# Hybrid decoder block on one core: eight of the FFN ends' LayerNorm tiles by ScalarE and POOL instead of two VectorE passes

## The chip, the cores and the metric

The kernel runs on one core of a Trainium2 chip. The metric is the device time of one execution in microseconds, taken as the median of several runs. Before the change the runs took 2291.83, 2285.61 and 2290.1 us, so the median is 2290.1 us.

Five engines work side by side on the core, each through its own instructions in order: PE (TensorE, matmuls and transposes), DVE (VectorE), ACT (ScalarE), POOL (GpSimd) and SP (SyncE, which here only issues DMAs). They wait for each other through semaphores.

## The reference

One decoder block over 1024 tokens of width 1024, with 16 learned meta tokens ahead of them, all in float32:

```python
h = layer_norm(ALPHA * h + 0.5 * swiglu(h, ffn1_w_gate, ffn1_w_up, ffn1_w_down), ln1_g, ln1_b)
h = layer_norm(ALPHA * h + hybrid_mixer(h, w_in, conv_w, w_att_out, w_conv_out, w_o), ln2_g, ln2_b)
h = layer_norm(ALPHA * h + 0.5 * swiglu(h, ffn2_w_gate, ffn2_w_up, ffn2_w_down), ln3_g, ln3_b)
return h[:, 16:]

def layer_norm(x, g, b):
    xc = x - mean(x)
    return xc * rsqrt(mean(xc * xc) + 1e-5) * g + b

def swiglu(x, w_gate, w_up, w_down):
    return (silu(x @ w_gate) * (x @ w_up)) @ w_down
```

The change touches the LayerNorm behind the first FFN and the one behind the second; the LayerNorm behind the mixer (ln2) stays.

## The kernel before, in words

**Stages.** The program runs FFN 1, the mixer, FFN 2. Tokens are worked on in tiles of 128: eight tiles t0 to t7 of 1024 tokens in all, and in FFN 1 a ninth tile, t8, with the 16 rows that are left over because of the meta tokens. Each FFN has a gate/up part, whose hidden values go to DRAM (`hd1` and `hd`), and a down projection, `halves_down`, which reads them back. Every float32 matmul is three matmuls on split values (`chain`, L262 to L269: high by high, high by low, low by high).

**The down projection.** `halves_down` multiplies by halves, with seven products P1 to P7 instead of eight. The hidden width is taken in chunks. For each chunk, for each half `ip` of the columns, and for each product, it lays the hidden values into a tile `hl` by DMAs that SP issues (L555; `load` runs some products ahead), multiplies them with the weights into a PSUM bank (tags a, b, c), and adds the bank to the tile's accumulator `y` on DVE (L595; L593 in the last chunk, where the row sums for the norm are taken along). In the last chunk, `ip` = 0 works on two column blocks at once: the tiles t0 and t1 are finished with product P3, t4 and t5 with P4. For `ip` = 1 each block is done by itself: t2, t6, then t3, t7. "First two tiles of each half" are t0, t1 and t4, t5.

**The norm behind it.** When a tile's last accumulation is through, `done` is called: `finish` at FFN 1, `done3` at FFN 2. Both call `short_norm` (L236 to L252): nm, the negative mean, on DVE (L243); Square with the row sum on ACT (L244); Sqrt on ACT (L245), ahead of whose first use a function table is loaded; z = (y + nm) * g on DVE (L246); r = 1/sqrt on DVE (L247); y = z * r + b on DVE (L250). Both long DVE passes read two tensors of 128x1024 in SBUF.

**What follows the norm.** At FFN 1, `finish` stores the tile to `h1` (L1222, DMA on SP) and then turns it for the mixer (`to_stream`, `turn`): per half of its columns four transposes on PE into a PSUM bank (L190), a cast on ACT (L191), the low part on DVE (L192). `done` holds these back: with the call for one tile, the first half of the tile two calls earlier is turned. At FFN 2, `short_norm` itself issues the store to the output (L252, on SP); nothing on PE reads the result.

**The longer form.** `layer_norm` (L219 to L234) is there already for some tiles of the mixer's norm: after r it computes nr = nm * r on DVE (L231), y = y * r + nr on ACT (L232, Identity), and then y * g and y + b as two passes on engines handed in (L233, L234).

**Who sets the order.** Code is written as generators, and a scheduler then sets the order of each engine's instructions from the whole program, so a change in one place also moves its neighbours. At run time each engine, SP's DMA queue among them, takes its instructions strictly in that order.

Of the kernel before, what the change touches and what calls it, by code (L numbers as in the profile page):

```python
# [11 lines left out]
F32 = mybir.dt.float32  # L12
# [3 lines left out]
AF = mybir.ActivationFunctionType  # L16
OP = mybir.AluOpType
# [3 lines left out]
D = 1024  # L21
# [69 lines left out]
class Block:  # L91
# [128 lines left out]
    def layer_norm(self, y, p, sums, gb, eng, junk, eps=None):  # L220

        eps = self.eps if eps is None else eps
        nc = self.nc
        g, b = gb
        new = lambda n: self.small.tile([128, 1], F32, name=n, bufs=6)[:p]
        nm, sq, ve, r, nr = new("nm"), new("sq"), new("ve"), new("rstd"), new("nr")
        nc.vector.tensor_scalar(nm, sums[:p, 0:1], sums[:p, 1:2], -1.0 / D, op0=OP.add, op1=OP.mult)
        nc.scalar.activation(junk[:p], y[:p], AF.Square, bias=nm, accum_out=sq)
        nc.scalar.activation(ve, sq, AF.Sqrt, bias=eps[:p], scale=1.0 / D)
        nc.vector.reciprocal(r, ve)  # L230
        nc.vector.tensor_tensor(nr, nm, r, OP.mult)  # L231
        nc.scalar.activation(y[:p], y[:p], AF.Identity, bias=nr, scale=r)  # L232
        eng[0].tensor_tensor(y[:p], y[:p], g[:p], OP.mult)  # L233
        eng[1].tensor_tensor(y[:p], y[:p], b[:p], OP.add)  # L234

    def short_norm(self, y, p, sums, gb, junk, z, parts=1, dst=None, eps=None):  # L236

        eps = self.eps if eps is None else eps
        nc = self.nc
        g, b = gb  # L240
        new = lambda n: self.small.tile([128, 1], F32, name=n, bufs=6)[:p]
        nm, sq, ve, r = new("nm"), new("sq"), new("ve"), new("rstd")
        nc.vector.tensor_scalar(nm, sums[:p, 0:1], sums[:p, 1:2], -1.0 / D, op0=OP.add, op1=OP.mult)  # L243
        nc.scalar.activation(junk[:p], y[:p], AF.Square, bias=nm, accum_out=sq)  # L244
        nc.scalar.activation(ve, sq, AF.Sqrt, bias=eps[:p], scale=1.0 / D)  # L245
        nc.vector.scalar_tensor_tensor(z[:p], y[:p], nm, g[:p], op0=OP.add, op1=OP.mult)  # L246
        nc.vector.reciprocal(r, ve)  # L247
        for j in range(parts):
            sl = slice(D // parts * j, D // parts * (j + 1))
            nc.vector.scalar_tensor_tensor(y[:p, sl], z[:p, sl], r, b[:p, sl], op0=OP.mult, op1=OP.add)  # L250
            if dst is not None:
                nc.sync.dma_start(dst[:, sl], y[:p, sl])  # L252
# [865 lines left out]
    def first_ffn(self):  # L1118

        nc, a = self.nc, self.a  # L1120
# [13 lines left out]
        with ExitStack() as c1:  # L1134
# [6 lines left out]
            with ExitStack() as c5:  # L1141
# [8 lines left out]
                y = []  # L1150
                for t in range(NT + 2):
                    p = 128 if t < NT else 8
# [62 lines left out]
            def finish(t, y, sums):  # L1215

                p = 128 if t < NT else 16
                junk = self.lnp.tile([128, D], BF16, name="junk")
                self.short_norm(y, p, sums, self.gb1, junk, self.lnp.tile([128, D], F32, name="z"), eps=self.eps4)
                if t < NT:  # L1220
                    r0 = META if t == 0 else 0
                    nc.sync.dma_start(self.h1[cols[t] + r0 - META:cols[t] - META + 128, :], y[r0:])  # L1222
                else:
                    for i in range(2):
                        nc.sync.dma_start(self.h1[512 + WIDE * i - META:520 + WIDE * i - META, :], y[8 * i:8 * i + 8])
                yield
                for half in range(2):
                    if half:

                        yield  # L1230
                    if t < NT:
                        self.to_stream(y, cols[t], 128, "ba"[half], (half,))
                        continue
                    ps = self.ps("ba"[half])
                    psv = ps.rearrange("q (j c) -> q j c", j=4)
                    for j in range(4):
                        nc.tensor.transpose(psv[:, j, :16], y[:16, 512 * half + 128 * j:512 * half + 128 * j + 128],
                                            self.ident[:16, :16])
                    for i in range(2):
                        hi, lo = (v[:, 4 * half:4 * half + 4, 512 + WIDE * i:520 + WIDE * i] for v in both)  # L1240
                        S.copy(hi, psv[:, :, 8 * i:8 * i + 8])
                        V.tensor_tensor(lo, psv[:, :, 8 * i:8 * i + 8], hi.bitcast(F32), OP.subtract)

            def done(t, y, sums):
                later.append(finish(t, y, sums))
                next(later[-1])
                if len(later) > 2:
                    next(later[-3])
# [13 lines left out]
    def run(self, stop=None):  # L1262
        nc, tc, a = self.nc, self.tc, self.a
# [14 lines left out]
        with ExitStack() as c2:  # L1278
            ys = ExitStack()
            yp = self.pool(ys, "f2y", 1, "right")  # L1280
            with ExitStack() as c3:
# [3 lines left out]
                y = []  # L1285
# [4 lines left out]
                gb = self.load_ln(lambda: wp.tile([128, D], F32, name="gb", bufs=2), a["ln2_g"], a["ln2_b"])  # L1290
# [22 lines left out]
                for t, (col, p) in enumerate(real):  # L1313
                    sums = self.small.tile([128, 2], F32, name="sums", bufs=6)
# [16 lines left out]
            with ExitStack() as c4:  # L1331
                up = self.weights_left(c4, 2, 2, 2)
                sp = self.pool(c4, "ws", 2)
                hps = ExitStack()
                with ExitStack() as c5:
                    tp = self.pool(c5, "f2t")
                    o1, o2 = real[0][0], real[NT // 2][0]
                    st1 = (self.xh, self.xl)
                    X = {"11": [x[:, 0:4, o1:o1 + 512] for x in st1], "21": [x[:, 4:8, o1:o1 + 512] for x in st1],
                         "22": [x[:, 4:8, o2:o2 + 512] for x in st1], "T1": [x[:, 0:4, o2:o2 + 512] for x in st1]}  # L1340
                    for n in ("T2", "T3", "T4"):
                        X[n] = [tp.tile([128, 4, 512], F32R, name=f"{n}{x}") for x in "hl"]
                    st = ExitStack()

                    gate_up.send((up, sp, X))
                    for g in later[NT - 2:]:
                        next(gate_up)
                        next(gate_up)
                        next(g, None)
                    for t in range(NT // 2):  # L1350
                        for n, src in (("T1", y[t][:, :512]), ("T2", y[t + 4][:, 512:]), ("T3", y[t + 4][:, :512]),
                                       ("T4", y[t][:, 512:])):
                            self.turn(src, 128, *(x[:, :, 128 * t:128 * t + 128] for x in X[n]), "c")
                            if t:
                                next(gate_up)
                    self.show("x3")
                    ys.close()
                    self.hp = self.pool(hps, "f2hl", 4, "right")
                    down = self.halves_down(up, sp, self.hd, wd, lambda t: [(0, self.h1[128 * t:128 * t + 128, :])])
                    next(down)  # L1360
                    pending = gate_up.send((self.pool(st, "f2h", 5, "right"), down))

                pools = {"more": self.pool(c4, "f2more", 4), "y": self.pool(c4, "f2y2")}
                rs = ExitStack()

                def ending():
                    st.close()
                    pools["r"] = self.pool(rs, "f2r", 1, "right")
                    self.lnp = self.pool(rs, "f2ln", 1, "right")
                    self.gb3 = self.load_ln(lambda: self.lnp.tile([128, D], F32, name="gb", bufs=2), a["ln3_g"], a["ln3_b"])  # L1370

                def done3(t, y, sums):
                    junk = self.lnp.tile([128, D], BF16, name="junk")
                    dst = a["out"][0, 128 * t:128 * t + 128, :]
                    z = self.lnp.tile([128, D], F32, name="z")
                    self.short_norm(y, 128, sums, self.gb3, junk, z, 1 if t < 7 else 2, dst, self.eps4)

                down.send((pending, pools, ending, done3))
                rs.close()
                hps.close()  # L1380
# [46 lines left out]
```

## Time and profile before

| | |
|---|---|
| median of 3 runs | 2290.1 us |
| the execution in the profile | 2288.11 us |
| its span, first to last instruction | 2286.3 us |
| mean granted TensorE clock | 0.977 of full speed |
| PE busy | 2192.2 us |
| DVE busy | 1530.8 us |
| ACT busy | 894.7 us |
| POOL busy | 841.0 us |
| FFN 1's first norm of a tile (DVE, nm) | at 718.24 us |
| FFN 2's first norm of a tile (DVE, nm) | at 2249.48 us |

Times inside the profile are microseconds from the span's start. A row of a timeline has the start, the duration, the engine and line, the operation with its output and inputs, and in brackets the idle time before it and what ended that. A row of waits names the waiting engine with its tile and line, and behind the arrow the engine and line whose result came last. DMA instructions are issued on SP's queue, called SPq. Starts of pipelined instructions may lie before the end of the one ahead.

### The profile page before, as it was taken

To read this page: it belongs to the slowest core of one execution; us is meant where nothing else is said; L and a number is where in the kernel's file an instruction comes from. 1 tells how busy PE (TensorE), PEld (TensorE's weight loads), DVE (VectorE), ACT (ScalarE), POOL (GpSimd) and SP (SyncE) were. 2 spreads that over 40 slices of the span, in tenths; PEclk is the share of its full clock that TensorE was granted. 3 is DMA by queue.
4 is the path that set the end of the run, shared out by engine and by line. 5 is a ranking of instruction groups with operands and counts; after the bars stand their busy time and mean duration, and the time that the engine had idled before them with its cause. 6 is when DMAs were issued, how large, how long until landed. Compare 5 with 4: busy or idle time off the path is not lost.

```text
span 2286.3 us, 31567 instructions
## 1 busy us (share of the span) xinstructions
PE 2192.2 (96%) x11708; PEld 1861.9 (81%) x11708; DVE 1530.8 (67%) x2716; ACT 894.7 (39%) x1484; POOL 841.0 (37%) x573
## 2 busy tenths in 40 slices
PE   6999999999999898999999999999999999989997
PEld 5999999987777777899887777777788888867776
DVE  6456565565787648699997787635555555555787
ACT  4434444443112327233225676432444444343212
POOL 2454555563220201265443110214355464653320
PEclk7999999999999898999999999999999999999999
DMA  3435445369685344431224212631253535368784
GB/s 121 133 109 160 145 127 178 102 230 333 196 269 173 106 136 93 130 76 43 74 83 97 51 42 70 221 143 65 65 184 118 186 105 190 112 225 308 236 272 155
DMA packets 299685, 335.02 MB, mean 147 GB/s; under 512 B 20432, under 2 KB 227948, under 8 KB 299148
## 3 DMA queue, kind: packets, MB, share of 16 engines
q1 hardware_dynamic: 230508, 243.33, 33.9%
q10 hardware_dynamic: 52976, 80.76, 9.9%
q0 software_dynamic: 16048, 8.93, 2.1%
q8 instruction: 92, 1.51, 0.3%
q14 instruction: 61, 0.50, 0.1%
HBM read 220.19 MB, written 112.76 MB: 146 GB/s over the span
## 4 chain that ended last, share of the span: by engine, by line
PE 52%; DVE 3%; DMA 3%; POOL 1%; ACT 1%; issue 1%; SPq 0%; DVEq 0%; ACTq 0%; POOLq 0%
PE a L269 14%; PE c L269 7%; PE ps L171 6%; PE ps L170 6%; PE ps L169 6%; PE b L269 3%; PE pt L958 2%; PE ps L1322 1%; PE ps L1323 1%; PE ps L1321 1%; PE po L949 1%; PE sc L923 1%; PE po L950 1%; DMA raw<-in_ffn_w_down_dram 1%; PE acc L760 1%
## 5 line engine op out<-in xcount | busy, mean ns | idle before, releaser
L143 DVE TENSOR_TENSOR lo<-raw,hi 128x1024 fp32r<-128x1024 f32 (+1 forms) x176 | 194.3, 1118 | 177.3 <-ACT hi L142 174.2
L142 ACT CAST hi<-raw 128x1024 fp32r<-128x1024 f32 (+1 forms) x219 | 187.9, 872 | 298.0 <-PE ps L170 81.6
L169 PE MATMUL ps<-xh,hi 128*128 128x512 f32 (+2 forms) x664 | 248.7, 375 | 0.3 <-DVE t L677 0.3
L171 PE MATMUL ps<-xh,lo 128*128 128x512 f32 (+2 forms) x664 | 248.5, 374 | 0.0
L170 PE MATMUL ps<-xl,hi 128*128 128x512 f32 (+2 forms) x664 | 248.3, 374 | 0.0
L793 DVE TENSOR_SCALAR_CACHE_REDUCE junk<-sc,cand 128x1040 uint8<-128x1040 f32 (+6 forms) x217 | 182.2, 893 | 0.0
L269 PE MATMUL c<-xh,hi 128*128 128x260 f32 (+1 forms) x704 | 176.0, 311 | 0.8 <-DVE T3l L192 0.8
L269 PE MATMUL c<-xh,lo 128*128 128x260 f32 (+1 forms) x704 | 176.1, 311 | 0.0
L269 PE MATMUL c<-xl,hi 128*128 128x260 f32 (+1 forms) x704 | 176.0, 311 | 0.0
L143 POOL TENSOR_TENSOR lo<-raw,hi 128x1024 fp32r<-128x1024 f32 (+1 forms) x43 | 87.9, 2044 | 207.8 <-ACT hi L142 207.8
L269 PE MATMUL a<-xh,hl 128*128 128x512 f32 x416 | 145.3, 398 | 4.6 <-DVE y L595 2.9
L323 POOL TENSOR_TENSOR ws<-raw 128x512 f32<-128x512 f32 x40 | 53.7, 1343 | 260.4 <-DMA raw<-in_ffn_w_gate_dram 202.1
L170 PEld LDWEIGHTS ps<-xl,hi 128*128 128x128 f32 x664 | 126.1, 190 | 17.0
L169 PEld LDWEIGHTS ps<-xh,hi 128*128 128x128 f32 x664 | 126.0, 190 | 16.8 <-DVE t L677 0.5
L171 PEld LDWEIGHTS ps<-xh,lo 128*128 128x128 f32 x664 | 125.7, 189 | 16.5
L595 DVE TENSOR_TENSOR y<-a,y 128x512 f32<-128x512 f32 x152 | 101.3, 684 | 39.6 <-PE a L269 39.2
L269 PE MATMUL a<-hi,hl 128*128 128x512 f32 x288 | 107.9, 420 | 20.2 <-DMA hl<-hd 8.3
L269 PEld LDWEIGHTS c<-xh,hi 128*128 128x128 f32 x704 | 114.5, 188 | 9.0 <-DVE T3l L192 1.0
L269 PEld LDWEIGHTS c<-xl,hi 128*128 128x128 f32 x704 | 114.6, 188 | 7.7
L269 PEld LDWEIGHTS c<-xh,lo 128*128 128x128 f32 x704 | 114.4, 188 | 7.8
L143 DVE TENSOR_TENSOR lo<-ws,hi 128x1024 fp32r<-128x1024 f32 x54 | 109.7, 2032 | 4.6 <-ACT hi L142 3.2
L269 PEld LDWEIGHTS a<-xh,hl 128*128 128x128 f32 x416 | 78.4, 188 | 25.4 <-DVE y L595 4.2
(360 smaller groups left out, 5892.6 us busy)
## 6 DMA issues: line engine op xcount, KB each, us to landing
hl<-hd SPq DMA_DIRECT2D x280, 256.0 KB
hd<-hl ACTq DMA_DIRECT2D x154, 256.0 KB
hd<-hl ACTq DMA_DIRECT2D x77, 512.0 KB
raw<-in_ffn_w_gate_dram SPq DMA_DIRECT2D x44, 512.0 KB
raw<-in_ffn_w_up_dram SPq DMA_DIRECT2D x44, 512.0 KB
raw<-in_ffn_w_down_dram SPq DMA_DIRECT2D x44, 512.0 KB
raw<-in_w_in_dram SPq DMA_DIRECT2D x37, 512.0 KB
h<-y SPq DMA_DIRECT2D x15, 512.0 KB
```

The lines of the kernel that those rows point to most:

```text
L142: self.nc.scalar.copy(hi, src)
L143: lo_eng.tensor_tensor(lo, src, hi.bitcast(F32), OP.subtract)
L169: mm(out, wh, xh, start=start, stop=False)
L170: mm(out, wh, xl, start=False, stop=False)
L171: mm(out, wl, xh, start=False, stop=stop)
L269: self.nc.tensor.matmul(out, w, v, start=start and first, stop=last, skip_group_check=True)
L323: P.tensor_tensor(s[:, 512:], r2[:, :512], r2[:, 512:], OP.add)
L595: V.tensor_tensor(yv, ps, yv, OP.add)
L760: nc.tensor.matmul(ps[:, :n], q[:, h, :], self.ki1[:, o:o + n], start=True, stop=False)
L793: V.tensor_scalar(junk[:, :x.shape[1]], x, s, None, op0=OP.is_ge, op1=OP.add, accum_out=cnt[:, j:j + 1])
L923: nc.tensor.matmul(ps[:, :w], q[:, r, :], self.k1[:, g, o:o + w], start=True, stop=False)
L958: nc.tensor.transpose(pt[:kw, m * r:m * r + m], ps_[r][q0:, 128 * kb:128 * kb + kw], self.ident[q0:, q0:])
```

## The change

A new function, `side_norm`, computes the norm in the longer form with three differences: nr on ACT instead of DVE, both passes with the weight g and the bias b on POOL, and no tile z. `finish` and `done3` call it for t0, t1, t4 and t5, and the other tiles keep `short_norm`. At FFN 2 the store of such a tile is issued by `done3` itself, in one piece as before. Over the whole program DVE loses 16 instructions, ACT and POOL have 16 more each, and PE and SP keep their number.

```diff
--- before.py
+++ after.py
@@ -232,6 +232,21 @@
         nc.scalar.activation(y[:p], y[:p], AF.Identity, bias=nr, scale=r)
         eng[0].tensor_tensor(y[:p], y[:p], g[:p], OP.mult)
         eng[1].tensor_tensor(y[:p], y[:p], b[:p], OP.add)
+
+    def side_norm(self, y, p, sums, gb, junk, eps):
+
+        nc = self.nc
+        g, b = gb
+        new = lambda n: self.small.tile([128, 1], F32, name=n, bufs=6)[:p]
+        nm, sq, ve, r, nr = new("nm"), new("sq"), new("ve"), new("rstd"), new("nr")
+        nc.vector.tensor_scalar(nm, sums[:p, 0:1], sums[:p, 1:2], -1.0 / D, op0=OP.add, op1=OP.mult)
+        nc.scalar.activation(junk[:p], y[:p], AF.Square, bias=nm, accum_out=sq)
+        nc.scalar.activation(ve, sq, AF.Sqrt, bias=eps[:p], scale=1.0 / D)
+        nc.vector.reciprocal(r, ve)
+        nc.scalar.mul(nr, nm, r)
+        nc.scalar.activation(y[:p], y[:p], AF.Identity, bias=nr, scale=r)
+        nc.gpsimd.tensor_tensor(y[:p], y[:p], g[:p], OP.mult)
+        nc.gpsimd.tensor_tensor(y[:p], y[:p], b[:p], OP.add)
 
     def short_norm(self, y, p, sums, gb, junk, z, parts=1, dst=None, eps=None):
 
@@ -1216,7 +1231,10 @@
 
                 p = 128 if t < NT else 16
                 junk = self.lnp.tile([128, D], BF16, name="junk")
-                self.short_norm(y, p, sums, self.gb1, junk, self.lnp.tile([128, D], F32, name="z"), eps=self.eps4)
+                if t in (0, 1, 4, 5):
+                    self.side_norm(y, p, sums, self.gb1, junk, self.eps4)
+                else:
+                    self.short_norm(y, p, sums, self.gb1, junk, self.lnp.tile([128, D], F32, name="z"), eps=self.eps4)
                 if t < NT:
                     r0 = META if t == 0 else 0
                     nc.sync.dma_start(self.h1[cols[t] + r0 - META:cols[t] - META + 128, :], y[r0:])
@@ -1372,8 +1390,12 @@
                 def done3(t, y, sums):
                     junk = self.lnp.tile([128, D], BF16, name="junk")
                     dst = a["out"][0, 128 * t:128 * t + 128, :]
-                    z = self.lnp.tile([128, D], F32, name="z")
-                    self.short_norm(y, 128, sums, self.gb3, junk, z, 1 if t < 7 else 2, dst, self.eps4)
+                    if t in (0, 1, 4, 5):
+                        self.side_norm(y, 128, sums, self.gb3, junk, self.eps4)
+                        nc.sync.dma_start(dst, y)
+                    else:
+                        z = self.lnp.tile([128, D], F32, name="z")
+                        self.short_norm(y, 128, sums, self.gb3, junk, z, 1 if t < 7 else 2, dst, self.eps4)
 
                 down.send((pending, pools, ending, done3))
                 rs.close()
```

The new order is shown at three places. The first is PE at the end of FFN 1 before the change, around the first transposes of t0 (tile `y0_5559`, first half, into bank b; `ident` is the identity matrix, `hl` the hidden values, `a` and `c` banks):

```order
L269 MATMUL a_7302<-hi_6834,hl_7100 128x512
L269 MATMUL a_7302<-xh_58,hl_7100 128x512
L269 MATMUL a_7302<-xl_59,hl_7100 128x512
L269 MATMUL a_7302<-xh_58,hl_7100 128x512
L269 MATMUL c_7335<-xh_58,hl_7160 128x512
L190 MATMUL b_7265<-ident_60,y0_5559 128x128 x4
L269 MATMUL c_7335<-xl_59,hl_7160 128x512
L269 MATMUL c_7335<-xh_58,hl_7160 128x512 x2
```

The same place on PE with the change (line numbers are 15 higher, and bank a_7302 is now a_7310):

```order
L284 MATMUL c_7343<-xh_58,hl_7160 128x512
L284 MATMUL a_7474<-hi_6834,hl_7307 128x512
L284 MATMUL a_7474<-lo_6835,hl_7307 128x512
L190 MATMUL b_7271<-ident_60,y0_5559 128x128 x4
L284 MATMUL a_7310<-hi_6834,hl_7199 128x512
L284 MATMUL a_7310<-lo_6835,hl_7199 128x512
L284 MATMUL c_7343<-hi_6911,hl_7180 128x512
L284 MATMUL c_7343<-lo_6912,hl_7180 128x512
L284 MATMUL c_7343<-hi_6911,hl_7180 128x512
L284 MATMUL c_7343<-hi_6954,hl_7180 128x512
```

Counted from the first matmul on hl_7100 (the one behind the products on hl_7083), 7 matmuls stood ahead of t0's transposes before, and 20 stand there now. The second place is PE a little later in the new order. Nine matmuls behind t0's transposes stand t1's (tile `y1_5560`), and 30 matmuls behind those t4's and t5's (`hm` holds the hidden values of the ninth tile):

```order
L621 MATMUL b_7361<-hi_6954,hm_112 48x512
L621 MATMUL b_7361<-lo_6955,hm_112 48x512
L190 MATMUL b_7394<-ident_60,y4_5563 128x128 x4
L284 MATMUL a_7474<-xh_58,hl_7307 128x512
L284 MATMUL a_7474<-xl_59,hl_7307 128x512
L190 MATMUL b_7424<-ident_60,y5_5564 128x128 x4
L284 MATMUL a_7474<-xh_58,hl_7307 128x512
```

Counted in matmuls from the same start, the first transposes of t0, t1, t4 and t5 stood behind 7, 18, 53 and 56 before, and stand behind 20, 29, 59 and 61 now.

The third place is SP's queue at the end of FFN 2 before the change (`out_0_dram` is the output, y0 to y7 are the tiles, `hl` the loads for the last products):

```order
L252 DMA out_0_dram<-y4_18811 128x1024
L555 DMA hl_20469<-hd_87 128x2x128 x2
L555 DMA hl_20480<-hd_87 128x2x128 x2
L252 DMA out_0_dram<-y5_18812 128x1024
L252 DMA out_0_dram<-y2_18809 128x1024
L252 DMA out_0_dram<-y6_18813 128x1024
```

and with it:

```order
L1395 DMA out_0_dram<-y4_18819 128x1024
L570 DMA hl_20485<-hd_87 128x2x128
L1395 DMA out_0_dram<-y5_18820 128x1024
L267 DMA out_0_dram<-y2_18817 128x1024
L570 DMA hl_20496<-hd_87 128x2x128 x2
L267 DMA out_0_dram<-y6_18821 128x1024
```

Both loads of the last `hl` tile (20480 before, 20496 now), which feeds the last product of the kernel, have moved from ahead of t5's store to behind it and t2's.

## Rows read from the trace of the kernel before

**Rows 1.** Page, part 1: busy time and share of each engine

```profile
PE 2192.2 (96%) x11708; PEld 1861.9 (81%) x11708; DVE 1530.8 (67%) x2716; ACT 894.7 (39%) x1484; POOL 841.0 (37%) x573
```

**Rows 2.** Busy time (instructions) of PE, PEld, DVE, ACT, POOL; granted clock; DMA share; GB/s

```profile
720.00:735.00 15.00, 15.00 (x73) 10.73 (x73) 14.83 (x28) 6.47 (x13) 0.00 (x0) 1.00 0.79 246
2266.00:2278.00 12.00, 8.81 (x31) 6.45 (x29) 11.02 (x23) 4.18 (x8) 0.00 (x0) 0.86 0.32 131
```

**Rows 3.** PE waits at FFN 1's end, 735 to 771: us, times, longest us

```profile
PE a L190 <- DVE xl L192: 1.8, 2, 1.5
PE b L190 <- DVE y L250: 1.7, 1, 1.7
PE b L190 <- DVE xl L1242: 1.3, 1, 1.3
PE pt L650 <- DVE xl L192: 1.2, 1, 1.2
PE b L190 <- DVE y L593: 1.1, 1, 1.1
```

**Rows 4.** PE waits at FFN 2's end, 2233 to 2287

```profile
PE a L269 <- DVE y L595: 2.9, 2, 2.4
```

**Rows 5.** Timeline of DVE, FFN 1's end: start us, us, line, operation [idle]

```profile
718.49 1.28 DVE L246 SCALAR_TENSOR_TENSOR z<-y,nm,gb 128x1024 f32<-128x1024 f32 x1
...
721.57 1.29 DVE L250 SCALAR_TENSOR_TENSOR y<-z,rstd,gb 128x1024 f32<-128x1024 f32 x1
...
732.07 1.28 DVE L250 SCALAR_TENSOR_TENSOR y<-z,rstd,gb 128x1024 f32<-128x1024 f32 x1
```

**Rows 6.** Timeline of ACT, FFN 1's end

```profile
721.25 1.13 ACT L244 ACTIVATE junk<-y,nm 128x1024 bf16<-128x1024 f32 x1
...
722.50 0.29 ACT L245 ACTIVATE ve<-sq,eps 128x1 f32<-128x1 f32 x1
```

**Rows 7.** Lines L232 and L234: ns min/median/max, first and last start

```profile
L232 ACT ACTIVATE y<-y,nr,rstd x6: 1243/1244/1245, 1507.8 to 1565.3; 128x1024 f32<-128x1024 f32 x6
...
L234 POOL TENSOR_TENSOR y<-y,gb x6: 2403/2416/3262, 1511.1 to 1567.9; 128x1024 f32<-128x1024 f32 x6
```

**Rows 8.** Timeline of PE, FFN 1's end

```profile
721.89 0.40 PE L269 MATMUL a<-hi,hl 128*128 128x512 f32 x1
...
723.06 0.60 PE L190 MATMUL b<-ident,y 128*128 128x128 f32 x4
723.42 0.48 PE L269 MATMUL c<-xl,hl 128*128 128x512 f32 x1
```

**Rows 9.** Timeline of SP, FFN 2's end

```profile
2254.12 0.35 SPq L252 DMA_DIRECT2D out_dram<-y  x1
2254.57 2.33 SPq L555 DMA_DIRECT2D hl<-hd  x4
```

**Rows 10.** DMA issues: count, KB each, median us to landing

```profile
q<-qs POOLq DMA_DIRECT2D x16, 256.0 KB, 3.3
...
qi<-qis POOLq DMA_DIRECT2D x7, 512.0 KB, 4.6
```

**Rows 11.** Timeline of POOL, 1570 to 1580

```profile
1574.42 1.29 POOL L1307 TENSOR_TENSOR y<-y,y 128x512 f32<-128x512 f32 x1
1575.79 2.16 POOL L1308 TENSOR_TENSOR y<-y,y 128x512 f32<-128x512 f32 x1
```

**Rows 12.** Timeline of DVE, 1570 to 1580

```profile
1574.92 1.87 DVE L246 SCALAR_TENSOR_TENSOR z<-y,nm,gb 128x1024 f32<-128x1024 f32 x1
```

**Rows 13.** Timeline of PE, FFN 2's end

```profile
2271.34 0.79 PE L269 MATMUL a<-hi,hl 128*128 128x512 f32 x1 [2.45 <-DVE y L595]
...
2274.07 0.63 PE L269 MATMUL c<-hi,hl 128*128 128x512 f32 x1
```

**Rows 14.** Timeline of DVE, FFN 2's end

```profile
2252.81 1.29 DVE L250 SCALAR_TENSOR_TENSOR y<-z,rstd,gb 128x1024 f32<-128x1024 f32 x1
...
2278.10 0.68 DVE L593 SCALAR_TENSOR_TENSOR y<-a,y 128x512 f32<-128x512 f32 x1
```

## The prediction

> **What bounds the kernel now.** I read the page first: PE is busy for 96% of the span, DVE for 67%, POOL for 37% [rows 1]. Only work that PE waits for can change the time, so I looked for PE's waits at the two places that the change touches. The table by stretches shows PE full (15.00 of 15.00 us) while FFN 1's first tiles are normalised, and DVE nearly so (14.83); in FFN 2's last stretch PE has 8.81 of 12.00 us [rows 2]. The waits say what ended PE's idle time: at FFN 1's end five DVE instructions, together 7.1 us [rows 3], at FFN 2's end a DVE accumulation, 2.9 us [rows 4]. So at both ends DVE comes last. The question is whether PE is still waiting for DVE once eight tiles go by ScalarE and POOL, or for POOL.
>
> Times are summed against the profiled execution (2288.11 us for a span of 2286.3). It lies 2.0 below the median 2290.1, against which I state results. About 0.3%, 6.9 us, is what a measurement of this kernel tells from no change.
>
> **What goes.** Eight tiles lose DVE's two long passes, z and y, 1.28 and 1.29 us each [rows 5]: 16 x 1.28 = 20.5 us of DVE time, in two portions of 10.3.
>
> **What comes, FFN 1.** The chain of a side tile is nm (DVE), Square, Sqrt, r (DVE), nr, Identity (ACT), then two POOL passes. For t0, nm, Square and Sqrt with its table load stay where they are; ACT then does t1's Square from 721.25 and is free for nr at 722.50 [rows 6]. nr is a 128x1 ACT instruction; the nearest is the Sqrt, 0.29 us [rows 6]. Identity is on the trace in another stage, 1.24 us, and so is POOL's pass over 128x1024, 2.42 us as a rule, 3.26 at the longest [rows 7]. So POOL begins at 722.50 + 0.30 + 1.24 = 724.05. Two passes with gaps of 0.08 between POOL instructions [rows 11] are 5.0 us a tile, and ACT's 3.1 us a tile (Square 1.25 [rows 6], Sqrt, nr, Identity) runs ahead of it. POOL is a queue of its own: t0 ready at 729.1, t1 734.1, t4 739.1, t5 744.1. Of the four y passes of before the first ended at 722.86, the last at 733.35 [rows 5]: 6.2 us lost on t0, 10.8 on t5. POOL was idle in this stretch [rows 2], so nothing else is delayed there.
>
> Who waits? PE works in order, and the order puts the transposes of t0, t1 and t5 earlier than POOL can serve them. The first matmul on hl_7100 began at 721.42 (two ahead of the row at 721.89), and the matmuls follow each other every 0.234 us: five between 721.89 and 723.06 [rows 8]. Now 20 of them stand ahead of t0's transposes: PE comes at 721.42 + 4.68 = 726.1 and **waits 3.0** until 729.1. Four transposes (0.36, from 723.06 to 723.42) and 9 matmuls later it comes at 731.6 and **waits 2.5** for t1. After 30 more it comes to t4 at 741.5, late enough; after two more, at 742.3, it **waits 1.8** for t5. Sum **+7.3**.
>
> What DVE gains here I set at nothing: its relief lies in the same stretch in which PE now stands for POOL. Of PE's waits for DVE afterwards, 1.3 and 1.1 [rows 3] might fall away (bound -2.4). t3's z and y now stand ahead of t7's last accumulation instead of behind it; that could let t3 go earlier by up to 1.8 (bound -1.8). After the waits the clock could fall: twice 1.3 at worst, which is what six slow matmuls cost more in FFN 2 [rows 13] (bound +2.6); and one DVE pass of the short ninth tile may fall into POOL's run (+0.9). FFN 1: +3.1 to +10.8.
>
> **What comes, FFN 2.** The same chain runs 1531.24 later (t0's y pass began at 2252.81 instead of 721.57 [rows 5, 14]), so POOL begins at 2255.3, and four tiles take it to 2275.3. No PE work reads these tiles, but SP does: it issues in order. In the trace the store of the first tile starts at 2254.12, as its y is done (2252.81 + 1.29 [rows 14]), and the loads of hl behind it only at 2254.57 [rows 9]. In the new order the store of t5 stands ahead of both loads of hl_20496, which the last six matmuls of the kernel need. Before, all loads were ahead of the store of t5.
>
> POOL won't keep its 20 us here, because the z and y of t2 and t6 fall into its run: four DVE passes that read two 128x1024 tensors. The trace has one such meeting: a POOL pass of 128x512 that takes 1.29 alone takes 2.16 while DVE's z, itself 1.87 instead of 1.28, runs beside it [rows 11, 12]. I take this 0.87 four times, +3.5: t5 is ready at 2278.8. (The Trainium skill, "SBUF — State Buffer", section "Who interferes with whom", says that VectorE with two SBUF inputs and GpSimd share a port pair as an exclusive lock, and the loser fully blocks. By that rule a POOL pass can lose a whole DVE pass: 4 x 1.28 = 5.1 instead of 3.5, and FFN 2's sum would be 1.6 larger; the rows agree, since there the POOL pass began when the DVE pass was partly done.)
>
> Then SP issues t5's store at 2278.9, t2's store, and the two loads, 0.45 to 0.58 apart [rows 9]: the first load starts at 2279.8. Its landing has no row. 256 KB took 3.3 and 512 KB 4.6 on another queue [rows 10]; from that I estimate 2.7 for 128 KB, with 2.0 and 4.6 as bounds. The last matmuls start at 2282.5, after a long idle time. After the 2.45 us idle of before they came 2.73 us per six, at a granted clock of 0.86 over that stretch [rows 2, 13]; so too here: done at 2285.3, and the last accumulation starts at 2285.4 instead of 2278.10 [rows 14]: **+7.3**. What follows it (t7's own norm, unchanged on DVE, and its store) keeps its 8.2 us. Bounds: +2.3 without interference, at full clock and with 2.0 for the landing; +12.4 with every POOL pass at 3.26 and a slow landing.
>
> Sum: 7.3 + 7.3 = **+14.6**, so 2288.1 + 14.6 = 2302.7 for the execution in the profile, **2305** against the median (+0.6%).
>
> (The Trainium skill, "GPSIMD Engine Reference", section "Engine selection", speaks against the change too: it puts element-wise two-input work about twice as slow on GpSimd as on VectorE, 2.56 from our 1.28. The measured 2.42 is 0.14 shorter, so its figure would add about 1.1 over a queue of eight passes.)
>
> **The rivals.**
> *DVE decides (faster).* Place: the waits for DVE at both ends. If POOL's results came ahead of PE, the relief would give back FFN 1's 7.1 [rows 3] and FFN 2's 2.9 [rows 4] with the slow matmuls behind it (six at 0.455 instead of 0.234, 1.3): 11.3, **2278.8**. For it: DVE is nearly full in both stretches [rows 2]. It decides if POOL has t0 ready by 726.1, so a pass would have to take 1.0 us; the row has 2.42 [rows 7]. Chance 0.04.
>
> *Only FFN 1 loses (no change).* If the last loads of FFN 2 came in time, FFN 2 would gain 4.2 while FFN 1 loses 7.3: **2293**. That needs t5 ready by 2267.5 (the load 4 us before PE's last group, itself earlier by the 4.2), so 1.5 us a pass against 2.42; or fewer matmuls behind the store than the order shows. Chance 0.08.
>
> *Interference everywhere (slower still).* Every POOL pass takes 3.26, as the longest did [rows 7]: 6.7 us a tile. FFN 1 waits 4.7, 4.2 and 5.1, +14; FFN 2 ends with t5 at 2281.9 instead of 2278.8, +10.3: **2314**. For it: DVE is full in both stretches; against it: five of six passes took about 2.42. Chance 0.10.
>
> That the change doesn't do what it says is out: the order shows the eight tiles on POOL.
>
> **How the numbers follow.** The forecast has 0.78. Its range from the bounds, +5.4 to +23.2, is 2295 to 2313; with the third rival, 2295 to 2314, which leaves out the first two (0.12). Faster by over 6.9 us: 0.04, the first rival. Within 6.9: 0.09, the second and the forecast's lowest edge. Slower: 0.87.
>
> **What would show it.** Right: in FFN 1's end PE waits of 1.5 to 3.5 us for POOL's y at the transposes (L190) of t0, t1 and t5, and POOL's passes back to back for 20 us or more; in FFN 2's end PE's longest wait ended by the load of hl, not by DVE, with SP's store of t5 issued near 2286 (2278.9 plus FFN 1's loss); passes of 2.42 on POOL except beside DVE's z and y of t2 and t6. Wrong: POOL passes near 1.3, or PE's waits still ended by DVE with the sums of before; or no wait for hl at the end, which would leave the second rival. If FFN 1 shows the waits but the mixer behind it starts no later, its slack took them.

## The result and the profile after

| | before | with the change |
|---|---|---|
| median of 20 runs | 2284.36 us | 2297.26 us |
| lowest to highest | 2277.42 to 2291.83 | 2290.76 to 2301.40 |
| ratio, 95% interval | | 1.0057 [1.0046, 1.0067] |
| span of the profiled execution | 2286.3 us | 2291.0 us |

The change makes the kernel slower by 0.57%, some 13.0 us (10.5 to 15.3 by the interval). The forecast was +14.6 us, 2305 with a range of 2295 to 2314. The median of before fell from 2290.1 with 3 runs to 2284.36 with 20, which is why the time lies lower in the range than the difference does.

The two profiled executions differ by 4.7 us only, since the parts that the change leaves alone vary from one execution to the next: the first nm of FFN 1 starts between 713 and 720 us in the profiles of this study, and from there on the long middle varies by 10 us. So I compare the two ends, each from its first nm. FFN 1's stretch goes from that nm to the first matmul of the mixer's key projection (PE `acc`, L169), FFN 2's to the end of the span.

| | before | with the change | forecast |
|---|---|---|---|
| FFN 1's stretch | 769.11 - 718.24 = 50.87 | 771.75 - 713.26 = 58.49 (+7.6) | +7.3 |
| FFN 2's stretch | 2286.3 - 2249.48 = 36.82 | 2291.0 - 2245.82 = 45.18 (+8.4) | +7.3 |

The key projection starts so in the trace of before:

```profile
769.11 0.66 PE L169 MATMUL acc<-xh,hi 128*128 128x346 f32 x1 [0.67 <-ACT hi L142]
```

The page of the changed kernel, part 1, against [rows 1]; then its table by stretches (columns as in [rows 2]):

```profile
PE 2187.7 (95%) x11708; PEld 1857.4 (81%) x11708; DVE 1516.9 (66%) x2700; ACT 904.6 (39%) x1500; POOL 886.4 (39%) x589
```

```profile
720.00:735.00 15.00, 11.28 (x41) 7.81 (x40) 4.22 (x10) 6.88 (x13) 14.77 (x7) 0.77 0.45 136
2266.00:2278.00 12.00, 5.24 (x12) 3.29 (x12) 6.67 (x11) 0.45 (x1) 8.59 (x3) 0.59 0.38 134
```

DVE lost 13.9 us and POOL gained 45.4, while PE's share went from 96% to 95%. The sixteen passes taken from DVE were 20.5 us in the prediction; 3.3 us of the difference come back at FFN 2, where three of the passes left to DVE take 1.77, 2.66 and 2.71 us instead of 1.28, and the rest isn't followed here. In the stretch in which PE was full before, it now works for 11.28 of 15.00 us at a granted clock of 0.77, and POOL is busy for 14.77. In FFN 2's last stretch PE works for 5.24 of 12.00 us instead of 8.81. Both first nm come earlier in this execution, by 5.0 and 3.7 us; with the windows shifted by as much, PE works for 11.28 of 15.00 and 5.43 of 12.00 us, so the reading stays.

What PE waited for longest at FFN 1's end, 690 to 790 (engine, tile and line, what came last: us, times, longest), against [rows 3]:

```profile
PE b L190 <- POOL y L249: 3.7, 2, 2.7
...
PE a L190 <- DVE xl L192: 2.4, 1, 2.4
PE a L284 <- DVE y L608: 2.3, 2, 1.3
```

and at FFN 2's end, 2230 to 2291, against [rows 4]:

```profile
PE a L284 <- DMA hl<-hd: 6.9, 2, 3.9
PE a L284 <- DVE y L610: 2.7, 1, 2.7
```

At FFN 1 the first cause is new: POOL's second pass, for PE's transposes. The waits for DVE there hardly change: all of them together are 8.3 us before and 7.6 with the change. At FFN 2 the DVE wait is still there with 2.7 (2.9 before), and 6.9 us for loads of `hl` have come on top.

### The profile page after: what moved, and what is told of

Same layout as the page of the kernel before. It is cut to its first block, busy times and chain, and to the rows that moved or that the text cites. A ratio compares the mean times of both kernels' runs of the same rounds, so it can differ in the third digit from the quotient of the medians.

```text
span 2291.0 us, 31597 instructions
## 1 busy us (share of the span) xinstructions
PE 2187.7 (95%) x11708; PEld 1857.4 (81%) x11708; DVE 1516.9 (66%) x2700; ACT 904.6 (39%) x1500; POOL 886.4 (39%) x589
## 4 chain that ended last, share of the span: by engine, by line
PE 51%; DMA 3%; DVE 3%; issue 2%; POOL 2%; ACT 1%; SPq 0%; POOLq 0%; DVEq 0%; ACTq 0%
PE a L284 14%; PE c L284 7%; PE ps L170 6%; PE ps L171 6%; PE ps L169 6%; PE b L284 3%; PE pt L973 2%; PE ps L1340 1%; PE ps L1341 1%; PE ps L1339 1%; PE po L964 1%; PE sc L938 1%; PE po L965 1%; DMA raw<-in_ffn_w_down_dram 1%; PE acc L775 1%
## 5 line engine op out<-in xcount | busy, mean ns | idle before, releaser
L169 PE MATMUL ps<-xh,hi 128*128 128x512 f32 (+2 forms) x664 | 248.1, 374 | 0.1
L169 PEld LDWEIGHTS ps<-xh,hi 128*128 128x128 f32 x664 | 125.7, 189 | 16.6 <-DVE t L692 0.4
L284 PE MATMUL a<-hi,hl 128*128 128x512 f32 x288 | 106.9, 417 | 23.4 <-DMA hl<-hd 10.3
L610 DVE TENSOR_TENSOR y<-a,y 128x512 f32<-128x512 f32 x152 | 101.3, 684 | 41.9 <-PE a L284 41.4
```

Of the source, the lines that this page charges most:

```text
L169: mm(out, wh, xh, start=start, stop=False)
L284: self.nc.tensor.matmul(out, w, v, start=start and first, stop=last, skip_group_check=True)
L610: V.tensor_tensor(yv, ps, yv, OP.add)
```

## Following the two chains in the trace after

FFN 1, DVE's first nm, the first and the last of POOL's eight passes, and PE's rows at t0, t1, t4, t5 and the key projection:

```profile
713.26 0.22 DVE L242 TENSOR_SCALAR nm<-sums 128x1 f32<-128x1 f32 x1
```

```profile
719.08 2.42 POOL L248 TENSOR_TENSOR y<-y,gb 128x1024 f32<-128x1024 f32 x1 [27.73 <-ACT y L247]
...
736.02 2.39 POOL L249 TENSOR_TENSOR y<-y,gb 128x1024 f32<-128x1024 f32 x1
```

```profile
723.98 0.66 PE L190 MATMUL b<-ident,y 128*128 128x128 f32 x4 [2.71 <-POOL y L249]
...
728.80 1.11 PE L190 MATMUL b<-ident,y 128*128 128x128 f32 x4 [1.01 <-POOL y L249]
...
737.79 0.60 PE L190 MATMUL b<-ident,y 128*128 128x128 f32 x4
...
738.82 0.63 PE L190 MATMUL b<-ident,y 128*128 128x128 f32 x4
...
771.75 0.42 PE L169 MATMUL acc<-xh,hi 128*128 128x346 f32 x1 [2.85 <-ACT hi L142]
```

POOL begins 719.08 - 713.26 = 5.82 us after nm; the forecast had 5.81. Its eight passes end at 738.41, 25.2 us after nm (forecast 25.9). PE comes to t0's transposes too soon and waits 2.71, and waits 1.01 for t1. It is in time for t4 and t5. From 723.98 to the wait before 728.80, that is to 727.79, PE needed 3.81 us for four transposes and 9 matmuls, which are 2.47 at the pitch of [rows 8] (one matmul every 0.234 us); from 728.80 to 737.79 it needed 8.99 for four transposes and 30 matmuls, 7.38 at that pitch. For a part of either stretch the matmuls follow each other every 0.43 us, so the lower clock after each wait cost 1.34 and 1.61. Waits and clock together are 6.7 of the 7.6 us; the rest is the balance of later waits, such as the 2.85 ahead of the key projection, 0.67 before, which I haven't followed one by one.

FFN 2, DVE's first nm and the last accumulation; six of POOL's eight passes; SP's stores of t4, t5 and t2 with the loads behind them; PE's two waits:

```profile
2245.82 0.22 DVE L242 TENSOR_SCALAR nm<-sums 128x1 f32<-128x1 f32 x1
...
2282.50 0.69 DVE L608 SCALAR_TENSOR_TENSOR y<-a,y 128x512 f32<-128x512 f32 x1 [3.66 <-PE a L284]
```

```profile
2251.64 2.41 POOL L248 TENSOR_TENSOR y<-y,gb 128x1024 f32<-128x1024 f32 x1 [26.20 <-ACT y L247]
...
2258.96 3.36 POOL L249 TENSOR_TENSOR y<-y,gb 128x1024 f32<-128x1024 f32 x1
2262.28 3.35 POOL L248 TENSOR_TENSOR y<-y,gb 128x1024 f32<-128x1024 f32 x1
2265.71 3.22 POOL L249 TENSOR_TENSOR y<-y,gb 128x1024 f32<-128x1024 f32 x1
2268.89 3.32 POOL L248 TENSOR_TENSOR y<-y,gb 128x1024 f32<-128x1024 f32 x1
2272.29 2.38 POOL L249 TENSOR_TENSOR y<-y,gb 128x1024 f32<-128x1024 f32 x1
```

```profile
2268.95 0.35 SPq L1395 DMA_DIRECT2D out_dram<-y  x1
2269.36 0.43 SPq L570 DMA_DIRECT2D hl<-hd  x1
2274.69 0.35 SPq L1395 DMA_DIRECT2D out_dram<-y  x1
2275.13 0.38 SPq L267 DMA_DIRECT2D out_dram<-y  x1
2275.61 2.02 SPq L570 DMA_DIRECT2D hl<-hd  x2
```

```profile
2272.33 0.79 PE L284 MATMUL a<-xh,hl 128*128 128x512 f32 x1 [3.87 <-DMA hl<-hd]
...
2279.56 0.76 PE L284 MATMUL a<-hi,hl 128*128 128x512 f32 x1 [3.03 <-DMA hl<-hd]
```

POOL again begins 5.82 us after nm. Four passes take 3.22 to 3.36 us instead of 2.4, +3.7 together (forecast: four times 0.87, +3.5). The last ends at 2274.67, SP issues t5's store at 2274.69, t2's at 2275.13, and the two loads behind them from 2275.61. PE's last group starts at 2279.56, 3.95 us after the first of these loads was issued, and the last accumulation at 2282.50: 36.68 after nm, against 2278.10 - 2249.48 = 28.62 before, so 8.1 later.

The longer of the two waits, 3.87 us, is the earlier one, and the prediction didn't have it. It hangs on t4's store: POOL's sixth pass ends at 2268.93, SP issues t4's store at 2268.95 and the load behind it at 2269.36, and PE starts 2.97 us later. It doesn't set the end, since PE then stands 3.03 us more for the loads behind t5's store.

## The experiments

All ratios are against the kernel before, in runs on the same chip. The table gives the two stretches from one profile each. How well a stretch repeats is seen where a kernel leaves an end as before: FFN 1's is 50.3 to 52.1 there, FFN 2's 35.9 to 36.9. (The expectations also speak of a mark in the mixer, 60.7 us from nm before; it is a matmul some 10 us behind the one used here.)

| kernel | side tiles | FFN 1's stretch | FFN 2's stretch | ratio, 95% interval |
|---|---|---|---|---|
| before | none | 50.87 | 36.82 | 1 |
| the change | t0, t1, t4, t5 at both ends | 58.49 | 45.18 | 1.0057 [1.0046, 1.0067] |
| ffn1_only | the four at FFN 1 | 58.29 | 36.79 | 1.0016 [1.0003, 1.0029] |
| ffn1_only_again | the same | 58.17 | 35.86 | 1.0027 [1.0014, 1.0040] |
| ffn2_only | the four at FFN 2 | 50.86 | 44.65 | 1.0036 [1.0020, 1.0052] |
| ffn2_pool_store | the four at FFN 2, stores by POOL | 50.31 | 39.24 | 1.0016 [1.0000, 1.0031] |
| no_bias | the four at both ends, without + b | 53.44 | 34.48 | 0.9996 [0.9981, 1.0012] |
| ffn2_no_pool | the four at FFN 2, without g and b | 52.09 | 33.68 | 0.9977 [0.9962, 0.9991] |
| ffn2_two | t0, t1 at FFN 2, stores by POOL | 51.79 | 37.89 | 1.0001 [0.9988, 1.0014] |
| ffn1_lag | the four at FFN 1, transposes later | 56.53 | 36.94 | 1.0008 [0.9994, 1.0022] |
| ffn1_t45 | t4, t5 at FFN 1 | 50.55 | 36.92 | 0.9976 [0.9962, 0.9990] |
| ffn1_t45_again | the same | 50.56 | 36.89 | 0.9997 [0.9984, 1.0010] |
| both_t45 | t4, t5 at both ends, stores by POOL | 50.55 | 35.18 | 0.9980 [0.9968, 0.9992] |

**One end at a time.** In `ffn1_only` the four tiles are taken out of `done3`, in `ffn2_only` out of `finish`:

```diff
-                    if t in (0, 1, 4, 5):
+                    if t in ():
                         self.side_norm(y, 128, sums, self.gb3, junk, self.eps4)
```

> side_norm at FFN 1's end alone; FFN 2's end as before. Theory (PE stands in order behind POOL's eight passes): the stretch from the first nm to the mixer's first groups is 7.5 us longer than before, as it was with the whole change, FFN 2's end is as before (36.8 us from nm to the end), and the kernel is 7 to 8 us slower (ratio 1.003). Rival (the loss at FFN 1 is taken back by slack in the mixer, all of the difference lies at FFN 2): within 2 us of before.

> side_norm at FFN 2's end alone. Theory (the stores of the side tiles stand on SP ahead of the last loads and wait for POOL): from nm to the end 45 us instead of 36.8, two long waits of PE for hl, the kernel 7 to 9 us slower. Rival (the two ends don't add, something common to both costs the time): the two single changes together differ from the whole change (12.9 us) by more than 4 us.

Each end is reproduced by itself: +7.4 us at FFN 1 with FFN 2 as before, +7.8 at FFN 2 with FFN 1 as before. In time that is +3.7 us (0.7 to 6.6) and +8.2 (4.6 to 11.9), 11.9 together against some 13 for the whole change, and the two stretches sum to +15.2 against +16.0. The intervals in time are wide, but by the stretches the ends add and the rival of a common cause falls. PE's new wait in the kernel with FFN 1 alone:

```profile
PE b L190 <- POOL y L249: 4.3, 3, 2.7
```

FFN 1's 3.7 us in time lies below its stretch, so I ran it again:

> The kernel with side_norm for all four tiles at FFN 1's end alone a second time, because its stretch is 7.4 us longer and its time only 3.7 us (interval 0.7 to 6.6). If the stretch decides, the ratio is 1.0025 to 1.004; if the mixer takes back half of it, 1.001 to 1.002.

The second time it was +6.2 us (3.2 to 9.1). The stretch's 7.4 is within the second interval and above the first. So FFN 1's loss is shown, and whether the mixer takes back a part of it isn't settled.

**The stores off SP.** Against `ffn2_only`, only the engine that issues the side tiles' stores is changed:

```diff
                     if t in (0, 1, 4, 5):
                         self.side_norm(y, 128, sums, self.gb3, junk, self.eps4)
-                        nc.sync.dma_start(dst, y)
+                        nc.gpsimd.dma_start(dst, y)
```

> side_norm at FFN 2's end alone, its four stores issued by POOL behind its own passes instead of by SP. Theory: PE's waits for hl vanish, though POOL's passes are as long and as late as ever; what is left is DVE's relief, up to 4.2 us at FFN 2's end, so 33 to 37 us from nm to the end, 0 to 4 us faster than before. Rival (POOL and DVE hold each other up, or the loads are slow by themselves): still 4 us or more slower than before, with passes of 3.3 us on POOL and PE's waits for hl.

PE's waits at FFN 2's end:

```profile
PE a L284 <- DVE y L610: 3.2, 1, 3.2
PE c L284 <- DVE y L610: 0.4, 1, 0.4
```

No wait for `hl` is left, though POOL is as slow as before: the stretch is 5.4 us shorter than with the stores on SP. That part of the theory holds. The other part doesn't: the relief was to bring the stretch to 33 to 37 us, and it is 39.24, 2.4 longer than before. PE waits for DVE again, 3.2 us, longer than before. So the rival was right in its first half, that POOL and DVE hold each other up. The rows of the two in that stretch show it:

```profile
2248.01 2.42 POOL L248 TENSOR_TENSOR y<-y,gb 128x1024 f32<-128x1024 f32 x1
2250.51 3.26 POOL L249 TENSOR_TENSOR y<-y,gb 128x1024 f32<-128x1024 f32 x1
```

```profile
2249.31 2.21 DVE L261 SCALAR_TENSOR_TENSOR z<-y,nm,gb 128x1024 f32<-128x1024 f32 x1
2251.44 0.68 DVE L608 SCALAR_TENSOR_TENSOR y<-a,y 128x512 f32<-128x512 f32 x1
...
2252.71 2.14 DVE L265 SCALAR_TENSOR_TENSOR y<-z,rstd,gb 128x1024 f32<-128x1024 f32 x1
...
2255.51 2.65 DVE L261 SCALAR_TENSOR_TENSOR z<-y,nm,gb 128x1024 f32<-128x1024 f32 x1
...
2258.74 2.72 DVE L265 SCALAR_TENSOR_TENSOR y<-z,rstd,gb 128x1024 f32<-128x1024 f32 x1
...
2264.94 2.79 DVE L261 SCALAR_TENSOR_TENSOR z<-y,nm,gb 128x1024 f32<-128x1024 f32 x1
```

POOL's pass from 2248.01 runs its 2.42 us, to 2250.43. DVE's z begins at 2249.31 and ends at 2251.52, 1.09 after POOL's end: by this it stood until POOL was through, then ran. Had the two shared a rate, POOL's pass would have been stretched too. POOL's next pass begins at 2250.51 and ends at 2253.77, 2.3 us after DVE's z: now POOL stood. DVE's y from 2252.71 again ends about 1.1 us after POOL's end, and so on. The five z and y passes that meet POOL take 2.21, 2.14, 2.65, 2.72 and 2.79 us, together 12.5 instead of 6.4 at 1.28 each. The accumulation at 2251.44, whose one input is a PSUM bank, takes its 0.68 as ever. So of the 10.3 us that DVE is spared, 6.1 come back in the passes that are left.

**How much POOL's length decides.** The next kernel leaves out POOL's pass + b, and so the bias b on the eight side tiles:

```diff
         nc.gpsimd.tensor_tensor(y[:p], y[:p], g[:p], OP.mult)
-        nc.gpsimd.tensor_tensor(y[:p], y[:p], b[:p], OP.add)
```

> The whole change, but POOL's second pass (+ b) is left out on the eight side tiles, so POOL's queue is half as long: 10 us instead of 20 at each end. Theory (the length of POOL's queue is the whole loss): FFN 1 loses at most 1.5 us, FFN 2 has its loads in time and gains up to 4; in all 0 to 6 us faster than before. Rival (the loss comes from the new order of the instructions, or from ACT's longer share, whatever POOL's length): still 6 us or more slower.

FFN 1's loss falls from 7.6 to 2.6 us, a little more than the 1.5 expected, with one wait for POOL of 1.2 left:

```profile
PE b L190 <- POOL y L248: 1.2, 1, 1.2
```

FFN 2's stretch is 2.3 us shorter than before, and the time is that of before. The rival (order or ACT) would have kept the loss. The order did move a little, since t0's transposes stand behind 16 matmuls in this kernel, 20 with the change and 7 before. Then both passes were left out at FFN 2 alone, to see the relief by itself:

> side_norm at FFN 2's end alone, without both of POOL's passes (the four side tiles stay without g and b), stores on SP as in the change. Theory: with POOL out of the way the stores are early, DVE's z and y take 1.28 us each, and the whole relief is seen: 32.5 to 34.5 us from nm to the end, 2 to 4 us faster than before. Rival (DVE isn't what ends last once PE is not held up, so its relief is worth nothing): 36 to 37 us.

The stretch is 33.68, 3.1 us shorter than before, as the theory had it; the time, 5.3 us less (2.1 to 8.7), leaves room for that and for more. PE's wait for DVE at this end, 2.9 us in [rows 4], is down to

```profile
PE a L282 <- DVE y L608: 0.8, 1, 0.8
```

So DVE does come last at FFN 2, and its relief is worth some 3 us, if POOL does nothing in exchange.

**Fewer tiles.** The short table of tiles is the only edit (`t in (0, 1)` at FFN 2, stores by POOL):

> side_norm for t0 and t1 alone, at FFN 2's end alone, stores by POOL. POOL then works for 10 us and is through before the short norms of t2 and t6 begin. Theory (what eats DVE's relief is that POOL's passes and DVE's two-input passes stretch each other): most z and y passes of DVE take 1.28 to 1.3 us again, the relief of 5 us stays, PE's waits for DVE (2.9 before) shrink, 33.5 to 36 us from nm to the end against 36.8 before and 39.2 with four tiles by POOL. Rival (ACT's share or the new order costs the time, not the meeting of POOL and DVE): 37 us or more.

This expectation failed: 37.89 us and a time like before's. I had looked at t2 and t6 only, but t4 and t5 keep the short norm here and come first. POOL began 7.1 us after nm and met t4's y, t5's z and y, and t2's z. DVE's passes there:

```profile
2256.84 2.16 DVE L265 SCALAR_TENSOR_TENSOR y<-z,rstd,gb 128x1024 f32<-128x1024 f32 x1
...
2259.52 2.80 DVE L261 SCALAR_TENSOR_TENSOR z<-y,nm,gb 128x1024 f32<-128x1024 f32 x1
...
2262.91 2.72 DVE L265 SCALAR_TENSOR_TENSOR y<-z,rstd,gb 128x1024 f32<-128x1024 f32 x1
...
2267.02 1.95 DVE L261 SCALAR_TENSOR_TENSOR z<-y,nm,gb 128x1024 f32<-128x1024 f32 x1
```

They add 4.5 us (9.63 against 5.12), nearly all of the 5.1 that DVE was spared. The mechanism stood, my placing of it was wrong.

At FFN 1 the same was tried with t4 and t5:

> side_norm at FFN 1's end alone and for t4 and t5 alone. Their transposes stand behind 50 and 56 matmuls, t0's and t1's (short norm) behind 7 and 18. Theory (PE stands for POOL only where the order asks for a tile sooner than POOL's queue gives it): both tiles are ready some 14 and 19 us after t0's nm, PE comes to them at 15 us or later, so its waits for POOL are under 2 us, and FFN 1's end is -2 to +2.5 us against before (60.7 us from the first nm to the mixer's mark). Rival (any tile on POOL costs, since POOL stretches DVE's passes for t0 and t1): +4 us or more.

POOL's first and last pass, and PE's transposes of t4 and t5:

```profile
724.64 2.43 POOL L248 TENSOR_TENSOR y<-y,gb 128x1024 f32<-128x1024 f32 x1 [30.15 <-ACT y L247]
...
732.00 2.40 POOL L249 TENSOR_TENSOR y<-y,gb 128x1024 f32<-128x1024 f32 x1
```

```profile
732.68 0.60 PE L190 MATMUL b<-ident,y 128*128 128x128 f32 x4
...
734.51 0.60 PE L190 MATMUL b<-ident,y 128*128 128x128 f32 x4
```

POOL has t4 ready at 729.56 and t5 at 734.40, and PE comes at 732.68 and 734.51: no wait for POOL, for t5 only just. DVE's z and y of t0 and t1 are through at 724.73, as POOL begins, and take 1.28 us each. The stretch is 50.55, like before's. The ratio 0.9976 promised more than the stretch gives, so this too was run again:

> The kernel with side_norm for t4 and t5 at FFN 1's end alone a second time, because its stretch (+0.8 us) and its time (ratio 0.998) pointed two ways. If the time is right, the ratio is again 0.996 to 0.999 and its gain lies outside the stretch; if the stretch is right, the ratio is 0.999 to 1.001.

The second ratio is 0.9997 and takes no gain for certain; the two intervals meet between 0.9984 and 0.9990. So no cost of two tiles at FFN 1 is seen; a gain of theirs isn't shown.

**The transposes later.** In `done` the lag is raised, so that a tile is turned two calls later:

```diff
-                if len(later) > 2:
-                    next(later[-3])
+                if len(later) > 4:
+                    next(later[-5])
...
-            for g in later[-2:]:
+            for g in later[-4:]:
                 next(g)
```

> side_norm for all four tiles at FFN 1's end alone, but done turns a tile five calls later instead of three, so the transposes of t0, t1, t4, t5 stand behind 44, 50, 56 and 80 matmuls instead of 20, 29, 59 and 61. Theory (place of the transposes against POOL's queue): POOL's waits shrink to t4's, up to 3 us, and FFN 1's end is 1 to 5 us longer than before instead of 7.4. Rival (the work that follows each tile has to be done anyway and only moves to the end): 7 us or more.

PE's transposes of t4 with their wait, and two of DVE's passes for the short ninth tile, t8:

```profile
736.35 0.66 PE L190 MATMUL b<-ident,y 128*128 128x128 f32 x4 [3.08 <-POOL y L249]
```

```profile
734.03 2.81 DVE L630 SCALAR_TENSOR_TENSOR y<-res,y 16x512 f32<-16x512 f32 x1
...
737.62 2.57 DVE L261 SCALAR_TENSOR_TENSOR z<-y,nm,gb 16x1024 f32<-16x1024 f32 x1
```

t0 isn't waited for at all, t1 for 0.34; 3.08 for t4 are left, as the count of matmuls said. The stretch is 5.7 us longer than before, past the 1 to 5 expected at this place (to the mixer's mark it is 5.8) and short of the rival's 7. All waits for POOL together fall only from 4.3 to 3.4 us. And a second cost has come in that the expectation had not counted: four of DVE's passes for t8, which in `ffn1_only` come behind POOL's run, now fall into it. They take 2.55, 2.81, 2.57 and 2.13 us instead of 0.67, 0.68, 1.26 and 1.26, so 6.2 more, and PE waits 3.1 us for DVE's accumulations (L610), which it didn't in `ffn1_only`. So this run mixes two causes, and how much of the loss the place of the transposes decides by itself isn't shown.

**Two tiles at both ends.** With t4 and t5 alone at both ends and stores by POOL:

> side_norm for t4 and t5 alone, at both ends, with POOL issuing their stores at FFN 2. Theory: at FFN 1 as in the kernel with those two alone; at FFN 2 all loads are ahead of late stores, DVE's passes for t0 and t1 are through before POOL begins and take 1.28 us, but POOL's 10 us may meet z and y of t2, two passes stretched by up to 1.5 each, against 5 us of relief: 34.5 to 37 us from nm to the end. Rival (POOL's meeting with DVE eats the relief in any arrangement): 37 us or more.

The ratio is 0.9980 [0.9968, 0.9992], 4.6 us faster than before, and by the two ratios some 17.6 faster than the change. FFN 2's stretch is 35.18, 0.7 below the shortest of those left as before. The two stretches account for 2.0 of the 4.6 us, and `ffn1_t45` had a like ratio once and didn't keep it. That this kernel beats the change is shown; that it beats the one before rests on one set of runs. DVE's pass for t1, and the three that meet POOL:

```profile
2246.90 1.27 DVE L265 SCALAR_TENSOR_TENSOR y<-z,rstd,gb 128x1024 f32<-128x1024 f32 x1
...
2253.10 2.43 DVE L261 SCALAR_TENSOR_TENSOR z<-y,nm,gb 128x1024 f32<-128x1024 f32 x1
...
2256.73 2.14 DVE L265 SCALAR_TENSOR_TENSOR y<-z,rstd,gb 128x1024 f32<-128x1024 f32 x1
...
2260.24 1.96 DVE L261 SCALAR_TENSOR_TENSOR z<-y,nm,gb 128x1024 f32<-128x1024 f32 x1
```

t1's y takes 1.27, since POOL hasn't begun. Three passes are stretched, by 2.7 us in all (6.53 against 3.84), against 5.1 of relief.

## Why the prediction was right

- **Who bounds.** PE's new waits are for POOL and for loads, as forecast. They don't replace the waits for DVE, which stay near 7.6 us at FFN 1 and 2.7 at FFN 2, but come on top of them. So the sign of being wrong, DVE's sums as before, nearly came about at FFN 1, beside the waits for POOL and not in their place; it fits the prediction's setting DVE's relief at nothing. The rival in which DVE decides needed POOL passes of 1.0 us; they took 2.4. The rival with interference everywhere needed passes of 3.26 at both ends; at FFN 1 all eight took 2.34 to 2.43, since DVE had no such pass beside them, and at FFN 2 four of eight were stretched.
- **FFN 1, +7.3.** The stretch shows +7.6, and POOL's start and end after nm came out within 0.7 us. The parts were shared out differently: I had waits of 3.0, 2.5 and 1.8 and took the clock for nothing, with 2.6 as its bound. Measured were waits of 2.7 and 1.0, none for t5, and 3.0 us of lower clock, above the bound, which made PE late enough for t5 and shortened the wait for t1. One and the same delay was paid in clock instead of in waits: in the two profiles of the kernel with FFN 1 alone the waits are 2.69, 0.48 and 1.14, and 2.68, 2.04 and none, and in all three profiles t5's transposes start 25.2 to 25.6 us after nm, where POOL's run ends at 25.1 to 25.2. DVE's relief, which I had set at nothing, didn't shorten the stretch.
- **FFN 2, +7.3.** Measured +8.1 at the last accumulation. SP's order was the mechanism, as `ffn2_pool_store` shows by undoing it alone. POOL's stretched passes were sized right (3.7 against 3.5). The landing was undersized: 3.95 us from the first load's issue to PE's start instead of 2.7. SP's issue of the two loads alone takes 2.02 us, where I had taken 0.45 to 0.58 between DMAs; the single load behind t4's store took 2.97. The store of t5 was to be issued near 2286 and was at 2274.69, because FFN 2 began some 11 us earlier in this profile than I had put it; after nm it is 28.9 us against 29.4. My lower bound of +2.3 adds up to +1.8 from its own terms, which doesn't move the range.
- **The second rival** (loads in time, FFN 2 gains 4.2) had its price wrong. With the loads in time FFN 2 still lost 2.4, because POOL stretches DVE's passes as DVE stretches POOL's, and I had priced that meeting on POOL's side only, although [rows 12] shows DVE's 1.87 for 1.28. In the change itself this is hidden behind SP's wait.
- **The sum, +14.6.** Measured 13.0 (10.5 to 15.3). The stretches of the two ends sum to 16.0 in the one profile. What lies between isn't settled, as FFN 1 by itself also showed less in time than in its stretch. So that the sum came within 1.6 us is in part luck: the stretches gave 1.4 more than forecast, and 3.0 less than that arrived in the time.

## What to carry to other kernels

Moving work from a busy engine to an idle, slower one cost time here wherever the result came later than the next engine in order asked for it; count the instructions ahead of the asking place, and compare with the slower engine's queue. A store that waited for late data held the loads behind it on SP; with such stores on the engine that makes the data, FFN 2's loss fell from 7.8 to 2.4 us. And POOL passes beside DVE passes that both read two SBUF tensors weren't two engines at work.

## What the runs showed of the hardware

DVE passes with two inputs in SBUF and POOL passes stood for each other in turn: 1.6 to 2.8 us for 1.28 on DVE, 2.7 to 3.4 for 2.4 on POOL, while accumulations from PSUM kept 0.68 beside the same POOL passes. This is what the Trainium skill states ("SBUF — State Buffer", section "Who interferes with whom": a DVE instruction with two SBUF inputs contends with GpSimd instructions that read SBUF, and the loser fully blocks). The stretched passes of the change lost 0.8 to 1.0 us each on POOL, 3.7 in all, where a whole DVE pass each would have made 5.1. Short DVE passes lost as much: those of 16 rows took 2.55 and 2.81 us instead of 0.67 in `ffn1_lag`. I hadn't expected the size of it: over a run of meetings it gave back between half and nearly all of the DVE time that the change had freed (6.1 of 10.3 us, 2.7 of 5.1, 4.5 of 5.1).

After waits of PE of 2.7 and 1.0 us the granted clock of the stretch was 0.77 of full speed, so it had been at the lower of its two levels (1.2 and 2.4 GHz) for part of it; that cost 3.0 us here, nearly as much as the waits themselves.
